# Hybrid mixer layer: the indexer's two query projections move into the modulation loop, the rotary tables ahead of it

## The chip, the cores and the metric

The kernel runs on one core of one Trainium2 chip. The metric is the device time of one execution in microseconds; lower is better. The core has five instruction streams that the profile names PE (TensorE, the matrix engine, with PEld for its weight loads), DVE (VectorE), ACT (ScalarE), POOL (GpSimd) and SP (here the queue that issues every DMA). Each works its queue strictly in order; an instruction that waits holds all that stand behind it.

## What is computed

One layer: a gated mixer of four causal branches on the same normalised and modulated input, and a gated convolutional feed-forward part. Sequence and width are 1024. For this change the first part of the mixer matters:

```python
mod = c_act @ ada_w[l] + ada_b[l]
sh1, sc1, g1, sh2, sc2, g2 = [m[:, None, :] for m in jnp.split(mod, 6, axis=-1)]
h = rmsnorm(x, mix_pre_g[l]) * (1.0 + sc1) + sh1
...
z = h @ w_in          # q, k, v of three attentions, conv input, qi, ki, wi, gates
...
q = rope(q, pos); k = rope(k, pos); qi = rope(qi, pos); ki = rope(ki, pos)
logits = jnp.einsum('bqhd,bkd->bqhk', qi[:, t0:t1], ki[:, :kl]).astype(jnp.float32) * IDX_HD ** -0.5
score = jnp.einsum('bqhk,bqh->bqk', jax.nn.relu(logits), wi[:, t0:t1])
score = jnp.where(jnp.arange(kl)[None, None, :] <= qpos[None, :, None], score, -jnp.inf)
_, idx = lax.top_k(score, topk)      # 256 keys for each query
```

The sparse attention then runs over the chosen keys alone. The indexer (qi, ki, wi) has eight heads of 32, so qi is 256 columns of `w_in`, two tiles of 128.

## The kernel before

All numbers stay in 32-bit precision by splitting: a matrix is written as a high and a low part (hH + hL for the input, whi + wlo for the weights), and a product is three matmuls, hH·whi, hL·whi and hH·wlo. `split_w` loads a weight tile of 128 columns (`wraw`), casts whi on ACT (L187) and subtracts on POOL to get wlo (L188). `proj` (L358) makes one tile: for each half of the sequence (512 positions) 24 matmuls, eight blocks of the contraction by three products, into one of the two buffers of `pmm`; then `consume` takes the half from PSUM. So one tile is 48 matmuls.

The program goes through these stages.

- **Head.** x comes in eight row tiles; each is scaled by its root mean square and transposed into xT (copies on DVE L313 and ACT L311). The modulation loop (L317) then has four steps m. In each, `ada_chunk` multiplies a 1024 x 512 piece of the modulation weights (four loads `adaw`, matmuls `adaps`, L205), ACT copies it (`adae`, L214), four small matmuls turn it into columns (`adac`, L217), and DVE forms `md`, A and B (L220 to L232). With these, two of the eight blocks of xT are scaled (DVE L320), cast to hH (ACT L322), and hL is the difference (DVE L323). After the loop come the rotary tables for two frequencies sets (`inv16`, `inv32`; DVE L326 to L338, sines on ACT L342 to L344) from the positions (`posi`).
- **Indexer.** `rope_tile` (L390) makes the two qi tiles: `proj`, two swapping copies on ACT (`sw`, L399 and L400), products with the tables on DVE (E=V; other rotary tiles use POOL), the cast `rhi` and the rest `lo` (kept in `sw`), and 16 row stores to a scratch in memory (`qk_s`, L123). `small_tile` (L416) makes ki together with wi; eight small transposes (`pw`, L453) need its `r`.
- **Scores.** For each of eight heads and six query blocks a score matmul (`sc<-kis,qis`, buffers `pss`, two of 1024), a relu on ACT and an accumulation on DVE. This part carries a higher priority than what stands behind it in the code.
- **Search.** A binary search over bits for the threshold of each query, on DVE (`search_v`, L607 to L620) and ACT (`search_a`, L634 to L638). Meanwhile TensorE works on the other projections: the plain tiles vc, vb, ua with the eight later modulation steps, then kdvd, qd, qc, kc, qb, kb. At its end DVE turns scores into masks (L674 to L679), and ACT writes them, one write for each of the query blocks 2 to 7 (`score<-key`, L680).
- **Sparse attention** (L690 to L730), in query blocks from 7 down: keys `kds` and queries `qds` are loaded from the scratch, score matmuls `sc<-kds,qds` (L468), maxima on DVE (`pd`, L710), exponentials on ACT (L719), transposes, and value matmuls (`av`, L488). Gate projections (32 tiles, `gate_tile`) fill TensorE from here on.
- **The rest**: stick-breaking attention with the causal convolution, differential attention, merge, and the feed-forward part.

No order is written out by hand. A scheduler places the instructions of all stages on the five queues, by priorities, by when buffers come free and by its own estimate of when each is ready; a change early in the program can therefore change the order far behind it.

## Time and profile before

| | us |
|---|---|
| median of 3 runs | 1996.43 |
| lowest, highest | 1993.14, 1999.46 |
| profiled execution | 1993.31 |
| span of its trace | 1991.5 |
| PE busy | 1809.1 (91% of the span) |
| DVE busy | 1284.8 (65%) |
| ACT busy | 913.2 (46%) |
| POOL busy | 770.3 (39%) |

The busy shares are means over stages that differ. Where a stage's limit lies is read from a window of the trace: the engine with hardly any idle time sets the pace there, and an engine with a hole in it tells in its timeline what it waited for. The timeline gives for each row the start, the duration, the engine, the line, the operation, the result and its sources, and in brackets the idle time ahead of it with what ended it.

### The profile page before, as it was taken

Reading aid. Unit: us, or ns where it says so; the run is one execution under the profiler, and the core shown is the slowest. Engines: PE = TensorE matmul, PEld = TensorE weight load, DVE = VectorE, ACT = ScalarE, POOL = GpSimd, SP = SyncE. Lnnn points to the kernel's source line nnn. Section 1 sums busy time; section 2 is a strip of 40 time slices with the busy share of each in tenths; the row PEclk is TensorE's granted clock in tenths of the full one; section 3 lists DMA queues with packets and bytes.
Section 4 is the critical chain, followed back from the end, with each engine's and each line's share of the span. In section 5 each row is a group of like instructions: output and inputs, shape, how many; then the busy total and the mean of one; then the engine's idle time right before and its main releaser. Section 6 shows DMA issues by size and latency. Waiting matters only on the chain.

```text
span 1991.5 us, 23311 instructions
## 1 busy us (share of the span) xinstructions
PE 1809.1 (91%) x8528; PEld 1403.5 (70%) x8528; DVE 1284.8 (65%) x1896; ACT 913.2 (46%) x1648; POOL 770.3 (39%) x425
## 2 busy tenths in 40 slices
PE   5888968399899999999999889869999999999998
PEld 3655656277677776767787667647888888778886
DVE  6758999704799865876313485577777777743532
ACT  5555757236546564555313344444444434343321
POOL 0202136273111111101214530198888888455450
PEclk9888989699999999989999989989999999999999
DMA  8355523343623224423223454312222222265631
GB/s 316 95 136 176 191 85 96 106 113 69 200 90 99 92 84 123 98 88 106 69 74 127 143 174 138 138 43 85 85 85 85 85 75 85 95 222 166 236 127 64
DMA packets 78306, 237.18 MB, mean 119 GB/s; under 512 B 10672, under 2 KB 14896, under 8 KB 78064
## 3 DMA queue, kind: packets, MB, share of 16 engines
q1 hardware_dynamic: 78192, 235.69, 36.9%
q8 instruction: 67, 1.10, 0.2%
q14 instruction: 47, 0.39, 0.1%
HBM read 179.82 MB, written 55.84 MB: 118 GB/s over the span
## 4 chain that ended last, share of the span: by engine, by line
PE 64%; DVE 21%; ACT 4%; issue 4%; POOL 3%; DMA 3%; SPq 0%; DVEq 0%; ACTq 0%; POOLq 0%
PE ups L963 19%; PE mm L367 18%; PE dps L1191 11%; DVE junkb L607 7%; PE brp L927 3%; PE av L488 3%; PE sc L468 3%; PE yps L1011 2%; DVE hc L874 2%; PE tr L478 2%; POOL wlo L188 1%; DMA x_s<-xt 1%; PE adaps L205 1%; DVE T L620 1%; DVE th L1101 1%
## 5 line engine op out<-in xcount | busy, mean ns | idle before, releaser
L188 POOL TENSOR_TENSOR wlo<-wraw,whi 128x1024 fp32r<-128x1024 f32 x104 | 267.5, 2577 | 858.5 <-ACT whi L187 822.3
L367 PE MATMUL mm<-hH,whi 128*128 128x512 f32 x864 | 356.6, 413 | 48.3 <-ACT whi L187 30.0
L367 PE MATMUL mm<-hH,wlo 128*128 128x512 f32 x864 | 352.0, 408 | 2.7 <-POOL wlo L188 2.6
L367 PE MATMUL mm<-hL,whi 128*128 128x512 f32 x864 | 353.8, 410 | 0.3 <-DVE hL L323 0.3
L963 PE MATMUL ups<-th,wblk 128*128 128x512 f32 x1320 | 316.0, 396 | 19.5 <-DVE ub L1143 7.4
L963 PEld LDWEIGHTS ups<-th,wblk 128*128 128x128 f32 x1320 | 251.2, 191 | 77.8 <-DVE th L1101 11.5
L367 PEld LDWEIGHTS mm<-hH,whi 128*128 128x128 f32 x864 | 168.1, 195 | 94.8 <-ACT whi L187 30.4
L367 PEld LDWEIGHTS mm<-hH,wlo 128*128 128x128 f32 x864 | 167.7, 194 | 41.5 <-POOL wlo L188 3.9
L187 ACT CAST whi<-wraw 128x1024 fp32r<-128x1024 f32 x122 | 127.4, 1048 | 148.2 <-DMA wraw<-in_w_dn 57.6
L367 PEld LDWEIGHTS mm<-hL,whi 128*128 128x128 f32 x864 | 168.6, 195 | 35.6 <-issue 2.6
L942 POOL TENSOR_TENSOR wblk<-wr,wblk 128x512 fp32r<-128x512 f32 x84 | 174.2, 2084 | 8.0 <-ACT wblk L941 8.0
L1205 DVE TENSOR_TENSOR actl<-actw,acth 128x512 fp32r<-128x512 f32 x42 | 65.0, 1573 | 105.1 <-ACT acth L1204 105.1
L607 DVE TENSOR_SCALAR_CACHE_REDUCE junkb<-key,cf 128x1024 bf16<-128x1024 uint16 (+3 forms) x124 | 117.3, 946 | 4.3
L963 PE MATMUL ups<-h2h,wblk 128*128 128x512 f32 x352 | 117.2, 395 | 0.0
L942 POOL TENSOR_TENSOR wblk<-wsum,wblk 128x512 fp32r<-128x512 f32 x66 | 100.0, 1517 | 35.8 <-ACT wblk L941 35.8
L1130 DVE SCALAR_TENSOR_TENSOR ub<-ub,pkt 128x1023 f32<-128x1023 f32 x44 | 64.1, 1458 | 67.7 <-ACT ub L1129 67.7
L1191 PE MATMUL dps<-wlo,acth 128*128 128x512 f32 x336 | 104.2, 390 | 2.1 <-POOL wlo L188 2.1
L1191 PE MATMUL dps<-whi,acth 128*128 128x512 f32 x336 | 104.0, 389 | 0.0
L941 ACT CAST wblk<-wr 128x512 fp32r<-128x512 f32 x88 | 54.3, 622 | 108.2 <-PE ups L963 83.7
L1191 PE MATMUL dps<-whi,actl 128*128 128x512 f32 x336 | 103.9, 389 | 0.0
L874 DVE SCALAR_TENSOR_TENSOR hc<-hpad,pkt,hc 128x1024 f32<-128x1024 f32 x60 | 84.3, 1409 | 0.0
L1132 DVE SCALAR_TENSOR_TENSOR ub<-ub,pkt 128x1022 f32<-128x1022 f32 x44 | 83.4, 1895 | 0.8
(591 smaller groups left out, 3422.4 us busy)
## 6 DMA issues: line engine op xcount, KB each, us to landing
wraw<-in_w_in SPq DMA_DIRECT2D x54, 512.0 KB, 3.9
adaw<-in_ada SPq DMA_DIRECT2D x48, 512.0 KB, 5.9
wr<-in_w_up SPq DMA_DIRECT2D x44, 512.0 KB, 3.4
wraw<-in_w_dn SPq DMA_DIRECT2D x44, 512.0 KB, 3.4
sg_s<-gt SPq DMA_DIRECT2D x44, 256.0 KB, 2.4
sgl<-sg_s SPq DMA_DIRECT2D x22, 512.0 KB, 3.4
act_s<-ub SPq DMA_DIRECT2D x22, 512.0 KB, 2.6
actw<-act_s SPq DMA_DIRECT2D x42, 256.0 KB, 4.2
```

The lines of the kernel that those rows point to most:

```text
L187: A.copy(hi, raw)
L188: (E or G).tensor_tensor(out=lo, in0=raw, in1=hi.bitcast(F32), op=OP.subtract)
L367: PE.matmul(ps, a[:, ks], b[:, k, cs], start=(n == 0), stop=(n == 3 * NK - 1))
L468: PE.matmul(ps[:, c0:c1], a, b[:, c0:c1], start=(si == 0), stop=(si == len(stacks) - 1 and not last))
L607: V.tensor_scalar(out=j[:, :n], in0=src, scalar1=scal, scalar2=None, op0=op, op1=OP.add, accum_out=dst[:, kc(t):kc(t) + 1])
L874: V.scalar_tensor_tensor(out=hc, in0=hpad[:, k:k + S], scalar=w(k), in1=hc, op0=OP.mult, op1=OP.add)
L942: E.tensor_tensor(out=b[:, 1], in0=r, in1=b[:, 0].bitcast(F32), op=OP.subtract)
L963: PE.matmul(ps, u[:, ks], v[:, k, :], start=(n == 0), stop=(n == 11))
L1130: V.scalar_tensor_tensor(out=u[:, 1:], in0=c[:, 0:S - 1], scalar=w(1), in1=u[:, 1:], op0=OP.mult, op1=OP.add)
L1132: V.scalar_tensor_tensor(out=u[:, 2:], in0=c[:, 0:S - 2], scalar=w(0), in1=u[:, 2:], op0=OP.mult, op1=OP.add)
L1191: PE.matmul(ps[:, cs], a[:, tl], b[:, cs], start=(chunk == 0 and n == 0 and i == 0), stop=(chunk == len(CH) - 1 and n == len(ops) - 1 and ...
L1205: V.tensor_tensor(out=lo, in0=raw, in1=hi.bitcast(F32), op=OP.subtract)
```

## The change

The loop over the four modulation steps moves behind the code of the rotary tables. Ahead of it the two qi weight tiles are split and two buffers of `pss` (the score banks) are taken. Within the loop, after each block j of hH and hL is made, 12 matmuls go into these two accumulators (two tiles, three products, two halves). `rope_tile` takes the finished accumulator in place of calling `proj`. The number of matmuls is the same.

```diff
             posi = stp.tile([P, S], I32, name="posi", tag="st")
             dma(posi, dap(pos, 0, [[0, P], [1, S]]))
-            for m in range(4):
-                mod_affine(m, A1, B1, "g1", pmm, "mm", stp, "st", adp)
...
             posf = stp.tile([P, S], F32, name="posf", tag="st")
...
                 tabs[kind] = (cs, sn)
 
+            qi_ps = []
+            for i in range(2):
+                qi_ps.append((pss.tile([P, S], F32, name="qips", tag="s"), split_w(w_in[W_INDEX[("qi", i)]])))
+            for m in range(4):
+                mod_affine(m, A1, B1, "g1", pmm, "mm", stp, "st", adp)
+                for j in (2 * m, 2 * m + 1):
+                    V.tensor_scalar(out=xT[:, j, :], in0=xT[:, j, :], scalar1=A1[:, j:j + 1],
+                                    scalar2=B1[:, j:j + 1], op0=OP.mult, op1=OP.add)
+                    A.copy(hH[:, j, :], xT[:, j, :])
+                    V.tensor_tensor(out=hL[:, j, :], in0=xT[:, j, :], in1=hH[:, j, :].bitcast(F32),
+                                    op=OP.subtract)
+                    ks = slice(j * P, (j + 1) * P)
+                    for ps, (hi, lo) in qi_ps:
+                        for n, (a, b) in enumerate(((hi, hH), (lo, hH), (hi, hL))):
+                            for hf in range(2):
+                                cs = slice(hf * 512, hf * 512 + 512)
+                                PE.matmul(ps[:, cs], a[:, ks], b[:, j, cs], start=(j == 0 and n == 0),
+                                          stop=(j == NK - 1 and n == 2))
...
-        def rope_tile(name, i, kind, nh, hd, scale=None, E=G):
+        def rope_tile(name, i, kind, nh, hd, scale=None, E=G, done=None):
...
-            proj(name, i, consume)
+            if done is None:
+                proj(name, i, consume)
+            else:
+                for hf in range(2):
+                    cs = slice(hf * 512, hf * 512 + 512)
+                    consume(hf, cs, done[:, cs])
             store_hl(name, i, hi, lo, nh, hd, True)
...
-            rope_tile("qi", i, "inv16", 4, 32, E=V)
+            rope_tile("qi", i, "inv16", 4, 32, E=V, done=qi_ps[i][0])
```

What this moves on the queues is seen at three places. The number behind a name tells one buffer from the next, and "..." stands for rows left out. Lines of the changed kernel are 11 to 16 higher from L318 on: L354 is the new matmul, L378 `proj`, L410 to L419 `rope_tile`, L484 a score matmul, L552 `hl_tile`, L696 the score write.

**TensorE in the modulation.** Before, the four steps follow each other; the first projection matmul (mm_494) stands behind the last:

```order
L217 MATMUL adac_321<-ones_66,adae_319 128x1 x4
L205 MATMUL adaps_337<-adaw_338,cst_c_99 32x512
...
L217 MATMUL adac_356<-ones_66,adae_354 128x1 x4
L205 MATMUL adaps_372<-adaw_373,cst_c_99 32x512
...
L217 MATMUL adac_391<-ones_66,adae_389 128x1 x4
L205 MATMUL adaps_407<-adaw_408,cst_c_99 32x512
...
L217 MATMUL adac_426<-ones_66,adae_424 128x1 x4
L367 MATMUL mm_494<-hH_117,whi_490 128x512
```

After:

```order
L217 MATMUL adac_365<-ones_66,adae_363 128x1 x4
L205 MATMUL adaps_405<-adaw_406,cst_c_99 32x512
...
L354 MATMUL qips_332<-hH_117,whi_335 128x512 x2
...
L354 MATMUL qips_339<-hL_118,whi_342 128x512 x2
L217 MATMUL adac_424<-ones_66,adae_422 128x1 x4
L205 MATMUL adaps_464<-adaw_465,cst_c_99 32x512
...
L354 MATMUL qips_332<-hH_117,whi_335 128x512 x2
...
L217 MATMUL adac_483<-ones_66,adae_481 128x1 x4
```

Between each two groups of adac there are now 24 matmuls of the two qi tiles, on the blocks that the step made.

**TensorE ahead of the scores.** Before, the last tile ahead of the first score matmul is the second plain tile (vc, block 1; mm_1175 and mm_1201 are its halves):

```order
L367 MATMUL mm_1175<-hH_117,whi_1171 128x512
...
L367 MATMUL mm_1201<-hH_117,whi_1171 128x512
...
L367 MATMUL mm_1201<-hH_117,wlo_1172 128x512
L468 MATMUL sc_774<-kis_766,qis_771 128x384
L468 MATMUL sc_779<-kis_766,qis_771 128x512
```

After, the third plain tile (vb, block 0; mm_1263 and mm_1289) follows it ahead of the scores:

```order
L378 MATMUL mm_1199<-hH_117,whi_1169 128x512
...
L378 MATMUL mm_1199<-hH_117,wlo_1170 128x512
L378 MATMUL mm_1263<-hH_117,whi_1259 128x512
...
L378 MATMUL mm_1289<-hH_117,whi_1259 128x512
...
L378 MATMUL mm_1289<-hH_117,wlo_1260 128x512
L484 MATMUL sc_772<-kis_764,qis_769 128x384
```

So 48 matmuls moved from behind the first score matmuls to ahead of them.

**ACT at the end of the search, and SP at the start of the sparse attention.** ACT before, from the last instruction of its search (T2) on; chi_2115 is kc, block 0:

```order
L638 ACTIVATE T2_2702<-Bn_2705 128x2
L680 ACTIVATE score_759<-key_2695,zcol_68 128x384
L536 ACTIVATE chi_2115<-mm_2151 128x512
...
L680 ACTIVATE score_759<-key_2695,zcol_68 128x896
L187 CAST whi_2187<-wraw_2185 128x1024
L187 CAST whi_2255<-wraw_2253 128x1024
L680 ACTIVATE score_759<-key_2695,zcol_68 128x1024
```

ACT after; chi_2181 is qc, block 1, and sw_2318 is qb, block 0:

```order
L654 ACTIVATE T2_2700<-Bn_2703 128x2
L552 ACTIVATE chi_2181<-mm_2217 128x512
...
L187 CAST whi_2253<-wraw_2251 128x1024
L187 CAST whi_2322<-wraw_2320 128x1024
L696 ACTIVATE score_757<-key_2693,zcol_68 128x384
...
L696 ACTIVATE score_757<-key_2693,zcol_68 128x896
L410 ACTIVATE sw_2318<-mm_2326 64x512
...
L696 ACTIVATE score_757<-key_2693,zcol_68 128x1024
```

Two weight casts moved from behind five score writes to ahead of all, and the projections are one tile further. SP before, around the last query load (qds) and the row stores of the last four rotary tiles (rhi, sw):

```order
L123 DMA qds_3435<-qk_s_81 64x1024 x2
...
L123 DMA wraw_6482<-in_w_in 128x1024
L123 DMA qk_s_81<-rhi_2321 16x1024 x8
...
L123 DMA qk_s_81<-rhi_2594 16x1024 x8
L123 DMA qk_s_81<-sw_2593 16x1024 x8
L123 DMA o_s_85<-oT_3438 128x1024
```

SP after:

```order
L123 DMA qds_3433<-qk_s_81 64x1024
L123 DMA qk_s_81<-rhi_2319 16x1024 x8
...
L123 DMA qk_s_81<-rhi_2592 16x1024 x8
L123 DMA qk_s_81<-sw_2591 16x1024 x8
L123 DMA qds_3433<-qk_s_81 64x1024
L123 DMA wraw_6480<-in_w_in 128x1024
```

The second half of the last query load and the first gate weights (wraw_6480) moved from ahead of the 64 row stores to behind them.

## Rows read from the trace of the kernel before

**Rows 1.** Windows: from:to, length; busy us (xcount) by engine; granted clock, DMA share, GB/s.

```profile
31.00:47.00 16.00, 11.51 (x71) 5.31 (x71) 13.39 (x24) 8.27 (x10) 0.00 (x0) 0.89 0.96 365
51.30:56.40 5.10, 5.10 (x13) 3.96 (x12) 5.10 (x9) 0.70 (x1) 1.50 (x1) 0.50 0.72 258
354.00:379.40 25.40, 0.01 (x1) 0.01 (x1) 24.74 (x37) 6.11 (x9) 1.34 (x1) 0.50 0.36 103
379.40:456.00 76.60, 70.15 (x291) 56.26 (x292) 7.56 (x3) 26.81 (x40) 54.18 (x35) 0.94 0.47 111
560.00:600.00 40.00, 35.94 (x188) 26.86 (x187) 39.73 (x46) 19.19 (x37) 5.30 (x2) 1.00 0.20 67
```

**Rows 2.** Timeline of DVE, end of the search.

```profile
353.68 0.16 DVE L620 SCALAR_TENSOR_TENSOR T<-ge,T 128x4 f32<-128x4 f32 x1
```

**Rows 3.** Timeline of PE, from the search to the attention.

```profile
379.39 0.79 PE L367 MATMUL mm<-hH,whi 128*128 128x512 f32 x1 [29.96 <-ACT whi L187]
...
455.42 1.99 PE L468 MATMUL sc<-kds,qds 128*128 128x512 f32 x8
...
465.47 1.97 PE L488 MATMUL av<-aT,vd 128*64 128x128 f32 x32
```

**Rows 4.** Timeline of ACT, score writes and the first rotary tile behind the search.

```profile
377.36 1.04 ACT L680 ACTIVATE score<-key,zcol 128x896 f32<-128x896 bf16 x1 [4.16 <-DVE key L679]
...
387.06 1.15 ACT L680 ACTIVATE score<-key,zcol 128x1024 f32<-128x1024 bf16 x1 [6.78 <-DVE key L679]
...
412.75 0.59 ACT L399 ACTIVATE sw<-mm 64x512 f32<-64x512 f32 x1 [3.65 <-PE mm L367]
```

**Rows 5.** Timeline of PE, two modulation steps.

```profile
30.03 1.05 PE L217 MATMUL adac<-ones,adae 128*128 128x1 f32 x8 [0.73 <-ACT adae L214]
...
35.22 1.05 PE L217 MATMUL adac<-ones,adae 128*128 128x1 f32 x8 [2.08 <-ACT adae L214]
```

**Rows 6.** Timeline of DVE, last x copy, modulation, tables.

```profile
25.94 0.69 DVE L313 COPY xT<-xtr 128x512 f32<-128x512 f32 x1 [1.31 <-PE xtr L308]
...
31.84 1.53 DVE L320 TENSOR_SCALAR xT<-xT,A,B 128x1024 f32<-128x1024 f32 x2
...
47.87 2.71 DVE L330 TENSOR_SCALAR ang<-posf,pkt 128x1024 f32<-128x1024 f32 x1
...
54.21 0.74 DVE L330 TENSOR_SCALAR ang<-posf,pkt 128x1024 f32<-128x1024 f32 x1
...
56.31 1.21 DVE L336 SCALAR_TENSOR_TENSOR ang<-kk,ang 128x1024 f32<-128x1024 f32 x1
```

**Rows 7.** Timeline of ACT, hH casts of a step and a sine.

```profile
32.69 1.99 ACT L322 CAST hH<-xT 128x1024 fp32r<-128x1024 f32 x2 [2.71 <-DVE xT L320]
...
63.91 1.15 ACT L342 ACTIVATE sininv<-ang,pkt 128x1024 f32<-128x1024 f32 x1 [0.69 <-DVE ang L338]
```

**Rows 8.** Chain that ended last, around M: start, length, what.

```profile
444.30 11.28 PE mm L367 x48
...
459.12 4.49 ACT pd L719 x8
```

**Rows 9.** Timeline of PE, second query projection.

```profile
69.39 0.79 PE L367 MATMUL mm<-hH,whi 128*128 128x512 f32 x1 [4.41 <-DVE r L402]
```

**Rows 10.** Timeline of POOL, weight remainders of the two qi tiles.

```profile
47.29 5.51 POOL L188 TENSOR_TENSOR wlo<-wraw,whi 128x1024 fp32r<-128x1024 f32 x2 [46.85 <-ACT whi L187]
```

**Rows 11.** Timeline of ACT, the key tile's last r copy.

```profile
98.33 0.57 ACT L433 COPY r<-mm 32x512 f32<-32x512 f32 x1 [1.87 <-DVE r L428]
```

**Rows 12.** Timeline of POOL, two rotary products of the last tile.

```profile
470.92 2.77 POOL L407 TENSOR_TENSOR r<-r,sw 128x512 f32<-128x512 f32 x2
```

**Rows 13.** Timeline of SP, row stores of the last rotary tile.

```profile
482.03 3.86 SPq L123 DMA_DIRECT2D qk_s<-rhi  x8
485.99 4.26 SPq L123 DMA_DIRECT2D qk_s<-sw  x8
```

**Rows 14.** Page, DMA issues: count, size, median us to landing.

```profile
wraw<-in_w_in SPq DMA_DIRECT2D x54, 512.0 KB, 3.9
```

More of the change, by code (lines that the diff above doesn't have):

```diff
@@ L316, in tile_hybrid_block @@
             dma(posi, dap(pos, 0, [[0, P], [1, S]]))
-            for m in range(4):
-                mod_affine(m, A1, B1, "g1", pmm, "mm", stp, "st", adp)
-                for j in (2 * m, 2 * m + 1):
-                    V.tensor_scalar(out=xT[:, j, :], in0=xT[:, j, :], scalar1=A1[:, j:j + 1],
-                                    scalar2=B1[:, j:j + 1], op0=OP.mult, op1=OP.add)
-                    A.copy(hH[:, j, :], xT[:, j, :])
-                    V.tensor_tensor(out=hL[:, j, :], in0=xT[:, j, :], in1=hH[:, j, :].bitcast(F32),
-                                    op=OP.subtract)
             posf = stp.tile([P, S], F32, name="posf", tag="st")
```

## The prediction

> **What bounds the kernel now.** I read the windows first, whole engines by stage, then the timeline of each engine where a window shows a hole. [rows 1] gives five stretches. From 31 to 47 us, the modulation, TensorE is busy 11.5 of 16 us and the DMA engines 0.96 of the time. From 51.3 to 56.4, the start of the first query projection, TensorE runs at half clock. From 354.0 to 379.4, right after the threshold search, it does nothing (0.01 us). From 379.4 to 456.0, the last six projection tiles, it is busy 70.2 of 76.6. From 560 to 600 VectorE is the bound with 39.7 of 40. So the kernel is a row of stages with different limits, and a saving in one counts only until the next stage that waits for something else. For this change I follow three points: T, the end of the threshold search (353.7, DVE, [rows 2]); M, the first score matmul of the sparse attention (455.4); and the first value matmul behind it (465.5) [rows 3]. From T on TensorE waits 29.96 us for a weight cast on ACT that stands behind five score writes there [rows 3, 4].
>
> **The modulation with the projections in it.** Before, four modulation steps follow each other on TensorE at 5.2 us (30.03 to 35.22, [rows 5]), and the two indexer projections (96 matmuls) come behind. After, the tables go first, and each next step's column matmuls (adac) stand behind 24 projection matmuls that need this step's hH and hL.
>
> The tables: per kind four plain passes, taken like the 0.74 of the product, and three fused steps of 1.21, so 6.6 us; with the int cast 13.9 for both [rows 6]. They can begin when the x copies end (25.94 + 0.69), so the first modulation column is used at about 41, where the first xT scaling began at 31.84 before [rows 6]: +10 at the columns. ACT's sines (1.15 each, four, and two absolute values, [rows 7]) stand ahead of and between the first hH casts, another 2 to 3 us; the first projection matmul can start at about 45. TensorE has been idle for over 10 us by then, so it begins at half clock, 0.43 us a matmul (12 in 5.1 us, [rows 1]): 14 of them slow (6.1 us, as in the trace), ten at 0.235 (11.28/48, [rows 8]), ends 53.5. Each further step is adac (1.05, [rows 5]), the four small DVE operations (0.7), one xT scaling (0.77, half of 1.53, [rows 6]), one hH cast (1.0, half of 1.99, [rows 7]) and 24 matmuls (5.6): 9.2 us. Three of them end at 81. In the kernel before the second tile began at 69.39, slow after a wait [rows 9], and its 48 matmuls, some ten at 0.43, end at about 82.5: the overlap is taken back by the tables and by the chain that now runs through TensorE, and the gain is some **1.5 us**. The weights are no limit: their two loads now stand right behind x.
>
> POOL's two weight remainders move with them, from 47.29 (5.51 us, [rows 10]) to beside the x scaling and the tables. The row of 47.87 shows what that does: the table product took 2.71 us beside POOL and 0.74 alone [rows 6]. Twice 2.0 is at most +4; VectorE has some 2.3 us of gaps among its last x copies, so I count +1 to +2 and have put it into the 41 above. The Trainium skill, page "SBUF — State Buffer", section "Who interferes with whom", says that VectorE and GpSimd share a port pair as an exclusive lock, so that the later one is fully blocked; the trace agrees (2.71 for 0.74), and by that rule alone, with no gaps to hide in, the sum below would be 2 us higher.
>
> **From the indexer to the scores.** The key tile (48 matmuls, 11.3 us, [rows 8]) then ends at about 92. The order on ACT now has the two r copies of this tile behind all six sw copies; the last one ended at 98.9 before ([rows 11], 5 us after the tile's last matmul), and 17 matmuls of the next tile stood between the two groups of transposes that need them. Now all eight transposes stand within the first two matmuls of that next tile, so TensorE waits 5 us at least, 6.6 with the six copies first (to about 98.5), and loses 2 more to the slow clock. And the order moves one whole plain projection tile (vb, block 0) ahead of the first score matmul: 48 matmuls, 11.3 us. Together −1.5 + 6.6 + 2 + 11.3 = 18.4, less some 1.4 of small waits of before in that stretch: the first score comes **+17 us** (+11 to +19). The scores are bound by VectorE and ACT, and the search by VectorE, so neither gets shorter: T moves by +17 too.
>
> **From T to M.** The tile that was moved ahead is missing behind the search: five tiles are left, not six, and the order puts the weight casts ahead of the score writes on ACT, so the 29.96 us wait goes. What is late next is the evacuation of the tiles between the score writes. The first half of the first rotary tile is evacuated behind the write of block 6, which ended at 377.36 + 1.04 = T + 24.7 [rows 4]; so at T + 25.5, where it was at 412.75 = T + 59.1. From there to M was 42.7 us (412.75 to 455.42). Its second half stands behind the write of block 7 (387.06 + 1.15 = T + 34.5) and the table load, some 11 us after the first, where 24 matmuls alone need 5.6 (half of 11.28, [rows 8]): +1 to +5, and I take +4. M is at T + 72 (25.5 + 42.7 + 4), before T + 101.7: **−30 us**.
>
> **From M to the attention.** On SP the second half of one query load (qds) and the next gate weights now stand behind the 16 row stores of the last rotary tile. Before, all query loads were issued ahead of those stores, and the stores went at 482.03 and 485.99, when nobody waited. TensorE's queue has a score matmul on that load in front of the value matmuls, and ACT has the cast of the gate weights in front of the next exponential, so both stand. The chain: the first exponential began at M + 3.7 and the value matmuls at M + 10 [rows 3, 8], so the first transposes are copied at an estimated M + 6.5 and the two r copies behind them end at M + 7.5; POOL's four pairs of rotary operations 5.4 (twice 2.7, [rows 12]); rhi and lo 1.9 until the stores can go on; 16 issues 3.86 + 4.26 = 8.1 [rows 13]; the load behind them 3.9 [rows 14]; the cast 1.0; then exponentials to the first value matmul 6.4 (459.12 to 465.47). That is M + 34 to 36, where it was M + 10.05: **+25 us**. No row of before shows SP's queue in that state, so the bounds are 0 (the load split lands before anyone needs it) and +30 (POOL locked beside VectorE's maxima, each operation like the 2.71 above).
>
> **Behind it** nothing is added: the same gate matmuls (1536) remain, some 28 more of them done when the first value block ends, and in the stretch from 560 on VectorE is the bound [rows 1], which takes what is left over. I count 0, with −5 to +3.
>
> **The sum:** +17 − 30 + 25 = +12. The profiled execution took 1993.31 us (span 1991.5), 3.1 below the median; on the median the forecast is 1996.4 + 12 = **2008**. Its own range is 2002.5 to 2018, from +23 to +27 for the stall, T + 69 to T + 74 for M, and 3 us either way at the head.
>
> **Rivals.**
> A faster one: the attention is not held. For it: no row of before shows the stall, it is read from SP's order alone, and a longer way to M would let the rotary work of the last tile go on before M. Against it: the POOL chain and the 16 issues stand ahead of the load and cannot be passed. It decides if the split load lands by about M + 10; then the 25 falls away: 2008 − 25 = 1983, and up to 1990 where part of it stays.
>
> A slower one: TensorE stays at half clock through the modulation steps. After each group of 24 matmuls it has only small matmuls until the next step. [rows 9] speaks for it: after an idle wait of 4.41 us the next projection began with 0.79 and 0.63 us matmuls, a granted clock of 0.5. Against it: the gap here is 3.6 us with eight modulation matmuls in it. It decides if each step starts slow: 24 at 0.43 in place of 0.235 is +4.7, three times, +14: 2022. The Trainium skill, page "TensorE: Matmul & The Clock Gate", section "HAM oscillation — how this bites in real kernels", describes just that, each short group starting cold after a wait; the trace agrees at 69.39, and no run here has the alternation yet.
>
> One without a difference: the head costs half. If the tables hide in the gaps of the x phase (they can start by tile, and x lands earlier when the modulation weights stand behind it), the first step is 5 us earlier, and the transposes find their copies in time (−5): +12 − 10 = 1998 to 2002.
>
> That the change does not do what it says is the case of the head itself: the projections do run inside the modulation, but their end moves by 1.5 us.
>
> **How the numbers follow.** Measurements of this kernel tell 0.3% from no change: 1990.4 to 2002.4. My forecast has 0.46, the slow clock 0.12, the head at half cost 0.19, the attention not held 0.23. Faster comes from the last alone, slower from the first two and a little of the third: faster 0.23, same 0.20, slower 0.57. To leave out no more than 2 in 10 the range must reach to the attention that isn't held and to the slow clock: 1981 to 2024.
>
> **What would show it.** In the new profile: the first projection matmul near 45 and the last near 81, in steps of about 9 us; the first score matmul about 17 us later; no hole in TensorE behind T; M at T + 72; then a hole of over 20 us in TensorE before the first value matmul, released by the query load. I am wrong if the steps are much shorter than 9 us, if the score matmuls start less than 8 us later, or if that hole is not there.

## The result, and the profile after

The changed kernel takes **2010.58 us** (median of six runs, 2005.66 to 2012.05); the kernel before takes 1997.13 in the runs beside it. The ratio is 1.0067 with a 95% interval of 1.0052 to 1.0081: slower by 13.4 us. The profiled execution of the changed kernel has a span of 2009.7 us, 18.2 more than before; the 4.8 us between the two differences come from the executions that were profiled (before's lies 3.8 under its median, after's 0.9 over).

The windows of the changed kernel, cut at its own first score matmul, end of the search, first score matmul M of the sparse attention and first value matmul; the next is the stretch of [rows 1] from 560; the last is everything behind the last gate tile. Columns as in [rows 1], with PE first and the granted clock after POOL.

```profile
0.00:139.86 139.86, 102.89 (x480) 75.92 (x481) 67.82 (x123) 57.80 (x91) 16.18 (x14) 0.90 0.53 167
139.86:382.96 243.10, 203.11 (x806) 138.31 (x805) 226.05 (x452) 159.25 (x375) 80.33 (x65) 0.87 0.45 149
382.96:456.63 73.67, 58.02 (x222) 45.00 (x220) 33.09 (x39) 26.97 (x40) 44.92 (x29) 0.91 0.35 76
456.63:494.05 37.42, 14.41 (x56) 10.40 (x54) 11.08 (x24) 12.48 (x21) 14.68 (x10) 0.64 0.60 164
...
560.00:600.00 40.00, 38.30 (x215) 28.46 (x214) 36.94 (x60) 18.38 (x52) 5.50 (x2) 1.00 0.43 125
963.40:2009.70 1046.30, 988.09 (x4237) 796.62 (x4235) 589.65 (x646) 396.67 (x591) 559.86 (x286) 0.98 0.33 114
```

The last row is the first thing to see: 1046.3 us, and behind the last gate tile of the kernel before it is 1045.9. By that tile is meant the last of the 22 gate tiles that run ahead of the merge (ten more follow in it); its milestone is the start of ACT's last copy of it. So the whole loss is made up to that tile, and up to there both kernels issue the same matmuls. T is the start of the search's last operation. The milestones (us from the span's start):

| | first score | T | M | first value matmul | last gate tile | span |
|---|---|---|---|---|---|---|
| before | 120.5 | 353.7 | 455.4 | 465.5 | 945.0 | 1991.5 |
| after | 139.9 | 382.8 | 456.6 | 494.1 | 962.8 | 2009.7 |
| difference | +19.4 | +29.1 | +1.2 | +28.6 | +17.8 | +18.2 |

TensorE in the changed kernel, the head and then the attention, with the wait and its end in brackets:

```profile
43.19 1.22 PE L354 MATMUL qips<-hH,whi 128*128 128x512 f32 x2 [8.88 <-ACT hH L346]
...
50.95 0.95 PE L217 MATMUL adac<-ones,adae 128*128 128x1 f32 x8
...
54.60 0.73 PE L354 MATMUL qips<-hH,whi 128*128 128x512 f32 x2 [0.83 <-ACT hH L346]
...
60.20 0.95 PE L217 MATMUL adac<-ones,adae 128*128 128x1 f32 x8
...
69.46 0.95 PE L217 MATMUL adac<-ones,adae 128*128 128x1 f32 x8
73.10 1.22 PE L354 MATMUL qips<-hH,whi 128*128 128x512 f32 x2 [2.70 <-ACT hH L346]
...
80.82 0.63 PE L354 MATMUL qips<-hL,whi 128*128 128x512 f32 x2
...
100.28 0.64 PE L469 MATMUL pw<-ctile,r 32*128 32x32 f32 x4 [6.24 <-ACT r L449]
...
393.74 0.80 PE L378 MATMUL mm<-hH,whi 128*128 128x512 f32 x1 [4.27 <-ACT czf L553]
...
456.63 1.31 PE L484 MATMUL sc<-kds,qds 128*128 128x512 f32 x5
...
481.81 1.62 PE L484 MATMUL sc<-kds,qds 128*128 128x512 f32 x3 [18.25 <-DMA qds<-qk_s]
...
494.05 1.97 PE L504 MATMUL av<-aT,vd 128*64 128x128 f32 x32
```

The projections run from 43.19 to 81.3, in steps of 9.25 us (50.95, 60.20, 69.46). The transposes `pw` wait 6.24 us. The hole behind the search, 29.96 us [rows 3], is gone; 4.27 us at 393.74 is the longest in its place. M comes 73.8 us after T instead of 101.7. And in front of the value matmuls stands the hole of 18.25 us, released by the query load. SP's queue in that stretch shows who holds it:

```profile
470.36 3.54 SPq L123 DMA_DIRECT2D qk_s<-rhi  x8
474.31 3.67 SPq L123 DMA_DIRECT2D qk_s<-sw  x8
478.03 0.45 SPq L123 DMA_DIRECT2D qds<-qk_s  x1
478.52 0.58 SPq L123 DMA_DIRECT2D wraw<-in_w_in  x1
```

And ACT in the same stretch:

```profile
468.50 0.62 ACT L419 CAST rhi<-r 128x512 fp32r<-128x512 f32 x1 [3.32 <-POOL r L418]
...
482.94 1.04 ACT L187 CAST whi<-wraw 128x1024 fp32r<-128x1024 f32 x1 [12.61 <-DMA wraw<-in_w_in]
485.82 1.15 ACT L735 ACTIVATE pd<-pd,sm 128x1024 f32<-128x1024 f32 x1 [1.83 <-DVE sm L734]
```

SP waits for the last rotary tile, issues its 16 rows (470.36 to 478), and only then the query half and the gate weights. ACT waits 12.61 us for these weights with the second exponential behind them.

One thing was not foreseen. The end of the search on VectorE:

```profile
373.05 0.90 DVE L635 TENSOR_TENSOR ge<-cnt,kreq 128x4 f32<-128x4 f32 x1
373.99 2.29 DVE L636 SCALAR_TENSOR_TENSOR T<-ge,T 128x4 f32<-128x4 f32 x1
376.32 2.29 DVE L632 TENSOR_SCALAR cf<-T 128x4 f32<-128x4 f32 x1
...
382.80 0.16 DVE L636 SCALAR_TENSOR_TENSOR T<-ge,T 128x4 f32<-128x4 f32 x1
```

POOL at the same time:

```profile
373.90 4.68 POOL L188 TENSOR_TENSOR wlo<-wraw,whi 128x1024 fp32r<-128x1024 f32 x2
```

Operations of four columns, 0.16 us at 382.80 and at the end of the search before [rows 2], take 2.29 beside two weight remainders on POOL. The search has 93 such small operations (31 steps of three). Before, 12 of them last over 0.3 us, after, 23, and every one of these lies beside an instruction on POOL. They add up to 28.9 us before and 38.8 after, while the counting passes between them take 127.6 us in both, and the search is 8.0 us longer (180.6 to 188.6). The longest stands in the kernel before, beside three rotary operations of POOL:

```profile
301.72 3.73 DVE L620 SCALAR_TENSOR_TENSOR T<-ge,T 128x4 f32<-128x4 f32 x1
```

The Trainium skill, page "SBUF — State Buffer", section "Who interferes with whom", says that a VectorE operation with two inputs in this memory contends with a GpSimd operation that reads it, over a port pair that is an exclusive lock; the trace agrees for T, which has two such inputs and was held almost a whole POOL subtraction (2.29 us of 2.36). cf, which reads one tile, was held as long at 376.32.

### The profile page after: what moved, and what is told of

Its sections match the earlier page's. It is cut to its first block, busy times and chain, and to the rows that moved or that the text cites. A ratio compares the mean times of both kernels' runs of the same rounds, so it can differ in the third digit from the quotient of the medians.

```text
span 2009.7 us, 23319 instructions
## 1 busy us (share of the span) xinstructions
PE 1813.9 (90%) x8528; PEld 1405.3 (70%) x8528; DVE 1288.9 (64%) x1896; ACT 915.0 (46%) x1648; POOL 769.8 (38%) x425
## 4 chain that ended last, share of the span: by engine, by line
PE 62%; DVE 21%; DMA 4%; ACT 4%; POOL 4%; issue 3%; SPq 1%; DVEq 0%; ACTq 0%; POOLq 0%
PE ups L979 19%; PE mm L378 16%; PE dps L1207 11%; DVE junkb L623 7%; PE sc L484 3%; PE av L504 3%; PE yps L1027 2%; PE tr L494 2%; PE brp L943 2%; PE qips L354 1%; DVE hc L890 1%; SPq L123 1%; DMA x_s<-xt 1%; POOL wlo L188 1%; DVE ge L635 1%
## 5 line engine op out<-in xcount | busy, mean ns | idle before, releaser
L378 PE MATMUL mm<-hH,whi 128*128 128x512 f32 x832 | 344.8, 414 | 27.8 <-ACT r L415 12.2
L378 PE MATMUL mm<-hH,wlo 128*128 128x512 f32 x832 | 340.0, 409 | 2.4 <-POOL wlo L188 2.4
L378 PE MATMUL mm<-hL,whi 128*128 128x512 f32 x832 | 341.4, 410 | 0.0
L979 PE MATMUL ups<-th,wblk 128*128 128x512 f32 x1320 | 314.3, 394 | 21.1 <-DVE th L1117 8.0
L378 PEld LDWEIGHTS mm<-hH,whi 128*128 128x128 f32 x832 | 162.1, 195 | 74.3 <-ACT r L415 15.0
L187 ACT CAST whi<-wraw 128x1024 fp32r<-128x1024 f32 x122 | 127.6, 1048 | 169.3 <-DMA wraw<-in_w_dn 56.7
L378 PEld LDWEIGHTS mm<-hH,wlo 128*128 128x128 f32 x832 | 161.4, 194 | 42.2 <-issue 5.8
L378 PEld LDWEIGHTS mm<-hL,whi 128*128 128x128 f32 x832 | 162.4, 195 | 34.2 <-issue 3.4
```

The source lines that it names most:

```text
L187: A.copy(hi, raw)
L378: PE.matmul(ps, a[:, ks], b[:, k, cs], start=(n == 0), stop=(n == 3 * NK - 1))
L979: PE.matmul(ps, u[:, ks], v[:, k, :], start=(n == 0), stop=(n == 11))
```

## The experiments

The theory, A: the change costs by what the scheduler's order did far behind it, namely the plain tile that it put ahead of the scores (later T) and the row stores that it put ahead of the query load and gate weights (the hole); and the head gains nothing since tables and chain eat the overlap. The rival, B: what such an order does is taken up elsewhere, by the work that is left over up to the gates, so that undoing it gives next to nothing, and the loss lies in the head. Their milestones in one table (profiled executions; ratio of the times to the kernel before that ran beside each, with interval). They come from one execution each, which lies 4.9 us over the median in e3, 5.8 over it in e6 and 3.7 under it in e7. In e2 and from e5 on the search's last operation lasts 2.29 us, so that the search ends 2.1 us later, against the other rows, than T says.

| | first score | T | M | value | last gate | us | ratio |
|---|---|---|---|---|---|---|---|
| after | 139.9 | 382.8 | 456.6 | 494.1 | 962.8 | 2010.6 | 1.0067 [1.0052, 1.0081] |
| e1 stores last | 138.6 | 379.7 | 455.1 | 478.4 | 952.3 | 2003.1 | 1.0033 [1.0022, 1.0043] |
| e2 tile back | 127.1 | 355.5 | 436.3 | 472.8 | 942.7 | 1990.2 | 0.9959 [0.9944, 0.9974] |
| e3 tables behind | 130.9 | 368.6 | 471.7 | 481.7 | 962.7 | 2007.3 | 1.0052 [1.0034, 1.0070] |
| e4 tables ahead | 119.6 | 355.4 | 457.2 | 467.3 | 946.8 | 1995.3 | 0.9998 [0.9986, 1.0010] |
| e5 both undone | 126.6 | 357.7 | 435.8 | 454.2 | 936.5 | 1984.2 | 0.9950 [0.9938, 0.9962] |
| e6 r first | 128.5 | 357.0 | 437.8 | 472.9 | 943.6 | 1989.0 | 0.9973 [0.9962, 0.9984] |
| e7 columns first | 123.5 | 351.9 | 429.9 | 467.3 | 935.6 | 1985.8 | 0.9959 [0.9947, 0.9971] |
| e8 all | 121.6 | 348.3 | 427.9 | 446.3 | 928.6 | 1979.4 | 0.9924 [0.9912, 0.9936] |
| e9 casts behind | 127.4 | 356.3 | 434.3 | 450.6 | 931.1 | 1981.8 | 0.9929 [0.9911, 0.9947] |
| e10 all, r not first | 122.8 | 351.1 | 429.1 | 445.5 | 926.1 | 1976.4 | 0.9904 [0.9890, 0.9919] |

### e1: the last tile's stores behind the loads

An issue order alone: the 16 stores of the last rotary tile (kb, 1) go behind the last query load of the first pair, and behind the first weights of the gates loaded there.

```diff
+    def behind(late, early):
+        for i in late:
+            tc.add_manual_dep(i.ins, early.ins.name, nosync, reason="issue order")
+    behind(stores["kb", 1], first_gate_weight_load)
+    behind(stores["kb", 1], last_query_load_of_pair_0)
```

> The changed kernel, with the 16 row stores of the last rotary tile queued on SP behind the second half of the last query load and the first gate weights; nothing else moves ahead of the sparse attention. Theory A (what TensorE stands idle before the gate projections end is paid in full): the 18.25 us wait for the query load goes, the first value matmul comes at about 470 in place of 494, and the kernel takes 1990 (1986 to 1994). Theory B (the stages behind give such a hole back, since the lag against the kernel before shrank from 27.6 us at the end of the sparse attention to 9 at the end of stick-breaking): not under 2005.

It gave 7.5 us (2003.1), between the two, and the intervals of the ratios do not overlap: the order of the stores does cost time, less than half of what A said. ACT of this kernel shows why:

```profile
467.01 0.62 ACT L430 CAST rhi<-r 128x512 fp32r<-128x512 f32 x1 [3.33 <-POOL r L429]
468.23 0.62 ACT L430 CAST rhi<-r 128x512 fp32r<-128x512 f32 x1 [0.60 <-POOL r L429]
468.76 1.04 ACT L189 CAST whi<-wraw 128x1024 fp32r<-128x1024 f32 x1
```

TensorE behind it:

```profile
469.85 0.80 PE L380 MATMUL mm<-hH,whi 128*128 128x512 f32 x1 [6.50 <-ACT whi L189]
...
478.35 1.97 PE L515 MATMUL av<-aT,vd 128*64 128x128 f32 x32
```

M to the value matmul shrank from 37.4 to 23.2 us, not to the 10 of before. ACT still has two casts ahead of the weights that wait for POOL, and the stores of the tile before (qb, 1), SP 450.32 to 457.6, still stood ahead of the load.

### e2: the plain tile back behind the first score matmul

```diff
-                    plain_tile(name, i, dst, func)
+                    with (tc.issue_after(first_score.ins) if (name, i) == ("vb", 0) else ExitStack()):
+                        plain_tile(name, i, dst, func)
```

> The changed kernel, with the third plain tile (vb, block 0) queued behind the first score matmul again; the query load still stands behind the row stores. Theory A: the first score matmul comes at about 128.5 (now 139.9), the search ends some 11 us earlier, M comes at 446 to 452 (now 456.6), and the kernel takes 2003 (1999 to 2007). Theory B (its 48 matmuls are only moved, and TensorE has no room for them in the search): M stays at 455 to 458 and the time at 2010, within 3.

It took away more than A said: 20 us against the changed kernel, and it beats the kernel before. First score 127.1, near the 128.5 expected; but the search ends 25.2 us sooner (27.3 by T) where the first score comes 12.8 sooner, and M comes 20.4 sooner. The edit does not put the tile back where the kernel before had it. There its first matmul stands behind 74 of the 80 score matmuls:

```profile
162.98 0.77 PE L367 MATMUL mm<-hH,whi 128*128 128x512 f32 x1
```

In e2 it stands behind two of them, and its last behind 46, while the next plain tile takes the late place:

```profile
127.48 0.40 PE L378 MATMUL mm<-hH,whi 128*128 128x512 f32 x1
```

So the run takes the tile from ahead of the scores and fills TensorE's waits among them with it, where neither kernel had one. The window of this kernel's scores stage shows one part (the granted clock is the third number from the end):

```profile
127.08:178.00 50.92, 46.96 (x177) 26.28 (x175) 42.99 (x59) 36.74 (x54) 5.35 (x5) 0.93 0.66 207
```

The same stage in the kernel before:

```profile
120.50:173.00 52.50, 44.26 (x129) 23.61 (x128) 44.05 (x54) 37.15 (x53) 8.48 (x6) 0.80 0.58 182
```

TensorE's granted clock is 0.5, the lower of its two levels, for 20.5 us of this stage before and for 23.9 in the changed kernel (mean 0.78 from 139.86 to 194), while the score matmuls wait for ACT and VectorE. With the tile's matmuls between them it is so for 6.8 us, TensorE does 48 matmuls more, and the stage is 4.1 us shorter than in the changed kernel (50.3 against 54.4; 52.6 before). So a tile placed there costs nothing; placed ahead, its 11.3 us stand in front of the first score. That the clock makes the stage shorter is not shown: 3.2 of the 4.1 us lie in the first seven heads, at 0.97 against 0.76, but in e5, with the same order and 0.93, these heads take as long as in the changed kernel (42.2 and 42.5 us; 39.3 in e2). The other part is the search, 180.4 us long by the end of its last operation instead of 188.7: its small operations add up to 29.8 us instead of 38.8, since POOL's work falls elsewhere.

That e2 beats the kernel before is therefore no proof for the change: one tile more is done by the end of the scores than there. The same edit on the kernel before was not run.

### e3 and e4: one half of the change alone

e3 keeps the projections in the loop and puts the tables behind it again; e4 is the kernel before with only the tables moved ahead. The edit of e3:

```diff
-            for kind in ("inv16", "inv32"):
...
             for m in range(4):
...
+            for kind in ("inv16", "inv32"):
...
```

and e4, against the kernel before:

```diff
+            for kind in ("inv16", "inv32"):
...
             for m in range(4):
...
-            for kind in ("inv16", "inv32"):
...
```

> One half of the change alone: the projections run block by block within the modulation loop, the rotary tables stay behind it as in the kernel before. By its order neither the extra tile ahead of the scores nor the split query load is there. Theory A: the first step begins at 34, not 43, the last projection matmul ends near 70 (now 81), the first score matmul comes at 110 to 116 (before 120.5), and the kernel takes 1989 (1985 to 1994). Theory B (the chain through adac takes the whole overlap back, as in the changed kernel): 1997, within 3.

> The other half alone: the rotary tables ahead of the modulation loop, the two projections behind it as in the kernel before; by its order neither the extra tile nor the split load is there. Theory A: the first modulation column is used at about 39 in place of 31, but the second projection no longer waits for VectorE's tables (4.4 us) and the first score matmul comes at 120 to 126; the kernel takes 1999 (1996 to 2003). Theory B (the tables cost their 10 us at the head in full): 2007, and most of the changed kernel's loss would be the tables.

Tables ahead cost nothing (0.9998, 1995.3 us, just under A's range): the first score is 0.9 us earlier, the rest within 2 us of before. The projections in the loop without them lose nearly as much as the whole change, some 10 us, and neither theory had that. TensorE of e3:

```profile
65.42 1.22 PE L333 MATMUL qips<-hH,whi 128*128 128x512 f32 x2 [5.25 <-ACT hH L325]
...
80.52 0.80 PE L377 MATMUL mm<-hH,whi 128*128 128x512 f32 x1 [6.45 <-ACT whi L187]
...
101.43 0.63 PE L468 MATMUL pw<-ctile,r 32*128 32x32 f32 x4 [5.11 <-ACT r L448]
```

The last two projection matmuls begin at 73.45, 7.4 us sooner than in the changed kernel. But the tables (VectorE up to 73.4, sines on ACT up to 78.2) stand between that and the rotary tiles, the next tile's weight cast on ACT comes behind the sines, and `pw` is at 101.43, later than with the tables ahead (100.28). Both kernels have the hole of before behind the search (TensorE idle 32.0 us from T to M in either). Read from these queues, what is gained at the projections is paid at the tables: they must go in one place or the other, and the chain from the last column to the key tile is no shorter. The first score is 10.4 us later than before, and scores and search take 4.5 us longer.

### e5: tile back and stores late together

e2, with the stores of (qb, 1) and (kb, 1) behind the query loads, and those of (kb, 1) behind the gate weights, as in e1.

```diff
+    behind(stores["kb", 1], first_gate_weight_load)
+    behind(stores["qb", 1] + stores["kb", 1], last_query_load_of_pair_0)
```

> The changed kernel with the tile back behind the first score matmul (as e2) and the row stores of the last two rotary tiles behind the query load, the last tile's also behind the first gate weights (e1 had left the tile before ahead of the load, and its hole was still 9.6 us). Theory A (TensorE's idle time up to the end of the gate projections is paid in full): against e2 the first value matmul comes 24 us earlier behind M (at M + 11 to 13), some 5 us of it are lost again where the second pair's query loads now stand ahead of gate weights, and the kernel takes 1973 (1969 to 1979). Theory B (half of such a hole comes back behind, as the gain of e1 may be read): 1983 or more.

1984.2 us, 0.9950: 26 us faster than the changed kernel, 11 slower than A had, and within B (1983 or more). By the medians the two effects nearly add up (20.4 and 7.5, 26.4 together); by the ratios, each against the kernel before beside it, the stores add less (0.9959 in e2, 0.9950 here, with overlapping intervals). A's sum failed twice. M to the value matmul is 18.4 us and not 11 to 13, with the queries in time; and of the 18.1 us that it is shorter than in e2, 6.2 are left at the last gate tile. That most of such a hole comes back is what B said; the section on the prediction shows where. ACT holds the second exponential behind two casts that wait for POOL:

```profile
447.69 0.62 ACT L430 CAST rhi<-r 128x512 fp32r<-128x512 f32 x1 [3.38 <-POOL r L429]
448.94 0.62 ACT L430 CAST rhi<-r 128x512 fp32r<-128x512 f32 x1 [0.63 <-POOL r L429]
449.46 1.15 ACT L754 ACTIVATE pd<-pd,sm 128x1024 f32<-128x1024 f32 x1
```

### e6: the key tile's r copies ahead of its sw copies (on e2)

```diff
             def consume(hf, cs, ps):
+                A.copy(r[64:96, cs], ps[0:32])
                 A.copy(sw[0:32, cs], ps[32:64])
...
-                A.copy(r[64:96, cs], ps[0:32])
```

> e2 with the key tile's two r copies ahead of its six sw copies on ACT. If the eight small transposes wait for these copies alone (theory A): they come at 95 in place of 98.5, the first score matmul 3.5 us earlier (at 123.5), and the kernel takes 1987 (1984 to 1989). If DVE's products of that tile set the pace of what follows: no change, 1990, within 1.

No change that can be told from e2: 1989.0 against 1990.2. The transposes come 2.6 us sooner (95.9), the first score 1.5 later (128.54). TensorE waits less for the transposes (6.25 us in e2), but now for the next tile, where e2 has no wait behind the transposes up to the first score:

```profile
95.90 0.31 PE L469 MATMUL pw<-ctile,r 32*128 32x32 f32 x2 [1.95 <-ACT r L441]
...
104.16 0.80 PE L378 MATMUL mm<-hH,whi 128*128 128x512 f32 x1 [2.86 <-DVE r L446]
```

So what TensorE must do before the first score counts, not the wait in front of `pw` alone; and its granted clock in the head was lower in this execution (0.89 against 0.92).

### e7: the next columns ahead of the projections (on e2)

In the code the projections of step m−1 come behind the modulation matmuls of step m, so that the chain to the next hH runs beside them.

```diff
             for m in range(4):
                 mod_affine(m, ...)
+                if m:
+                    qi_blocks((2 * m - 2, 2 * m - 1))
                 scale and cast blocks 2m, 2m+1
-                24 projection matmuls of blocks 2m, 2m+1
+            qi_blocks((6, 7))
```

> e2 with the modulation in step by one: the next step's column matmuls are traced ahead of this step's 24 projection matmuls, so that the DVE and ACT chain of a step runs beside the projections of the step before. Theory A (the step is 9.2 us because chain and projections add up): steps of 6 to 6.5, the last projection matmul at 69 (79 in e2), the first score matmul at 118, the kernel 1981 (1977 to 1986). Theory B (something else sets the pace of the steps, loads of the modulation weights or DVE): steps of 8 or more and 1988 to 1991.

Between the two: steps of 8.5 us instead of 9.25, as B had them, the first score 3.6 us sooner than in e2, the time (1985.8) inside A's range and 4 us less by the medians, but the same ratio to the kernel before, so the gain is not shown in the time. TensorE:

```profile
53.98 1.94 PE L205 MATMUL adaps<-adaw,cst_c 128*32 128x512 f32 x16
...
55.85 0.73 PE L348 MATMUL qips<-hH,whi 128*128 128x512 f32 x2
...
56.88 0.95 PE L217 MATMUL adac<-ones,adae 128*128 128x1 f32 x8
```

The modulation matmuls of the next step stand behind the last group of projections that the queue had, and copy, columns, scaling and cast follow (hH at 59.43), so that chain still takes part of each step.

### e8: all of it

e7, with the one table that the indexer needs ahead of the loop and the other behind it, the r copies first as in e6, and the stores as in e5.

```diff
-            for kind in ("inv16", "inv32"):
+            def table(kind):
...
+            table("inv16")
...
             for m in range(4):
...
+            table("inv32")
```

> All of e5, e6 and e7 together, and of the tables only the indexer's own frequencies ahead of the loop, the other table behind it (7 us less on DVE ahead of the first step). If the gains add (theory A): the first projection matmul at 37, the first score matmul at 108 to 111, the kernel 1955 (1948 to 1964). If the head's gains are lost again at a common wait (theory B: the search ends no earlier, since scores and key tile wait for DVE's products): 1970 or more.

1979.4 us, 0.9924, faster than both kernels and on B's side. A's 1955 was not reached: the last two projection matmuls begin at 70.04 and `pw` at 88.84, 11.4 us sooner than in the changed kernel, but the first score, at 121.6, is only 5.5 sooner than in e2. TensorE of e8:

```profile
88.84 0.44 PE L490 MATMUL pw<-ctile,r 32*128 32x32 f32 x4
...
97.93 0.63 PE L390 MATMUL mm<-hH,whi 128*128 128x512 f32 x1 [2.87 <-DVE r L467]
```

The wait has moved from the transposes to the next tile, whose bank the key tile still holds.

### e9: two casts behind the second exponential (on e5)

Again an order alone: on ACT the two `rhi` casts of (kb, 1) go behind the exponential of pair 0, block 7, second head.

```diff
+                ex = A.activation(p_[:, :n], src[:, :n], AF.Exp, bias=sm[:, 1:2], accum_out=sm[:, 2:3])
+                if (pr, t, hh) == (0, NT - 1, 1):
+                    behind(rhi_casts["kb", 1], ex)
```

> As the run with both parts undone (the plain tile back behind the first score matmul, the last tile's stores behind the query loads), and in addition the two rhi casts of the last rotary tile stand on ACT behind the second exponential of the attention. In that run the second exponential began at 449.46, held by two casts that waited 3.38 and 0.63 us for POOL's r, while its scores were done some 5 us earlier. Theory A, the rest of the hole before the first value matmul is the order on ACT: the first value matmul comes 4 to 5 us sooner behind M (13.5 to 14.5 us instead of 18.4), and the time falls by 3 to 5 us, to 1979 to 1981 against 1984 (ratio about 0.993). Theory B, VectorE's maxima and POOL's rotary work beside each other hold it: M to the value matmul stays 17 to 19 us and the time stays at 1984 (0.995).

M to the value matmul fell by 2.0 us, to 16.4; the last gate tile came 5.4 us sooner. The time, 1981.8 against 1984.2, is 0.2% lower; the intervals (0.9911 to 0.9947 and 0.9938 to 0.9962) overlap, so the time alone doesn't settle it. ACT, the second exponential:

```profile
444.87 1.15 ACT L756 ACTIVATE pd<-pd,sm 128x1024 f32<-128x1024 f32 x1 [2.05 <-DVE sm L755]
```

TensorE, the first value matmul:

```profile
450.64 1.97 PE L519 MATMUL av<-aT,vd 128*64 128x128 f32 x32 [1.47 <-ACT aT L512]
```

The exponential now waits for VectorE's maximum (`sm`), not for the casts. So the order on ACT was part of the rest of the hole, less than the 4 to 5 us that A gave it; M to the value matmul was 10.05 us before, and the other 6 are not resolved.

### e10: all of it, with the r copies back and the casts late

e8 without the edit of e6, and with that of e9.

```diff
-                A.copy(r[64:96, cs], ps[0:32])
                 A.copy(sw[0:32, cs], ps[32:64])
...
+                A.copy(r[64:96, cs], ps[0:32])
...
+                    behind(rhi_casts["kb", 1], ex)
```

> As the run with all parts (columns first, half of the tables ahead, the plain tile back, the stores late), but the key tile's r copies stand behind its sw copies again, and the two rhi casts of the last rotary tile behind the second exponential. Theory A, the r copies in front delayed the key tile's rows and with them the first score: the first score comes at 117 to 119 (121.6 with them in front), the value matmul 4 us sooner behind M, time 1972 to 1975 (ratio 0.988 to 0.990). Theory B, the first score hangs on the tables of the key tile and not on this order, and the casts give nothing: first score at 121 to 125, time 1979 to 1981 (0.992).

1976.4 us, **0.9904**, the fastest here: 19 us less than the kernel before beside it (1995.8) and 34 less than the changed kernel. A's reason falls: without the r copies in front the first score is at 122.8 and not at 117 to 119. TensorE, as in e6, pays for the transposes or for the next tile:

```profile
94.79 0.63 PE L492 MATMUL pw<-ctile,r 32*128 32x32 f32 x4 [5.12 <-ACT r L472]
...
122.84 0.56 PE L509 MATMUL sc<-kis,qis 128*128 128x384 f32 x2
```

B's time (1979 to 1981) falls as well. The value matmul comes 16.3 us behind M, 2.1 less than in e8, as in e9.

## Why the prediction was right, step by step

The sign was right, and so were the mechanisms that it named: the overlap taken back, the tile ahead of the scores, the hole behind the search gone, the new one in front of the value matmuls. That the time came out within 3 us (2008 against 2010.58) is luck: up to the value matmul the sum is 16.6 us short (+12 against +28.6), behind it it is 10.4 too high, and the two cancel.

| step | predicted | measured |
|---|---|---|
| projections in the loop | from 45 to 81, steps of 9.2 | from 43.2 to 81.3, steps of 9.25 |
| wait of the transposes | 6.6, then slow | 6.24, then 0.63 us a pair up to 105.7 |
| first score | +17 | +19.4 |
| scores and search get longer by | 0 | +9.8 (scores 1.8, search 8.0) |
| T | +17 | +29.1 |
| T to M | 72 (−30) | 73.8 (−27.9) |
| M to the value matmul | 34 to 36 (+25) | 37.4 (+27.4) |
| sum at the value matmul | +12 | +28.6 |
| behind it | 0 (−5 to +3) | −10.4 |
| whole | +12 | +18.2 in the span, +13.4 in the medians |

**The head** came as worked out: the overlap of projections and modulation is taken back (TensorE is idle 37.0 us up to the first score, 26.3 before). e4 shows that the tables cost nothing where they were put when the projections stay behind, and e3 that the projections in the loop gain nothing when the tables don't go ahead. The term of +1 to +2 for POOL's remainders is in the trace (the position cast took 2.25 us beside them, 0.69 alone in the kernel before). Two sums of the forecast do not come out as said: 26.6 and 13.9 make 40.5, so that the 41 holds half a microsecond of that term, and the lower end of its own range, 2002.5, is not what the bounds beside it add up to (2000).

**The tile ahead of the scores** was costed at 11.3 us, and as a shift that the stretch behind the search gives back. It did so: T to M is 27.9 us shorter. What e2 adds is that among the score matmuls the same tile would have cost nothing.

**"Neither gets shorter"** left out that they can get longer, and is the first step that was mis-sized. The sum had VectorE's search as a fixed length; its 8 us more are small operations beside POOL, set by what POOL does in that stretch. The 1.8 us of the scores are not resolved.

**T to M and the hole** came as read from the order: no hole of 30 us, and a new one, by the row stores. e1 shows the stores as a cause (37.4 to 23.2 with them late); the terms of the chain, POOL's pairs, the stores, the load and the cast, are all there: 464.77, 470.36, 478.03, 482.94. What the prediction left out is that with the stores away the rest does not fall to 10: e5 and e9 stand at 18.4 and 16.4.

**"Behind it nothing"** is the second, off by 10.4 us. The forecast had some 28 gate matmuls more done by the first value block and gave them no worth. In fact, at the end of the sparse attention (546.5 us before, 574.1 after) 75 gate matmuls were done before and 118 after, 10 of these in front of the first value matmul; and the value stage took no longer for it (81.0 and 80.0 us), since they fill its waits (TensorE is idle 7.1 us in it before, 1.3 after). From there to the last gate tile the kernel before takes 398.5 us and the changed one 388.8. So the 43 matmuls come back as 9.7 us. The other runs bear it out: with 75 (e3, e4, e5, e8 to e10) that stretch takes 397.4 to 398.5 us, with 118 (e2, e6, e7) 388.3 to 389.9, with 102 (e1) 396.7. This is also, in part, why the late stores cost less than the hole that they make. VectorE, which the forecast had as the bound from 560 on, is busy 36.9 of 40 us there after, and TensorE 38.3.

**Counting another way** shows both. Up to the last gate tile TensorE does the same matmuls, so its end moves by TensorE's idle time and by how long it is busy with them. Idle: 128.0 us before, 137.6 after, by stage (to the first score, the end of the search, M, the value matmul, behind it):

| | head | to T | to M | to value | behind | sum | busy |
|---|---|---|---|---|---|---|---|
| before | 26.3 | 41.8 | 32.0 | 1.7 | 26.2 | 128.0 | 816.9 |
| after | 37.0 | 40.0 | 15.7 | 23.0 | 21.9 | 137.6 | 825.2 |
| e2 | 39.3 | 36.0 | 13.9 | 22.1 | 21.1 | 132.5 | 810.2 |
| e5 | 38.0 | 36.9 | 13.9 | 7.0 | 27.0 | 122.8 | 813.7 |

9.6 us of idle time and 8.3 of slower matmuls are the 17.8 at the last gate tile. The head is worth +10.7, and not the first score's +19.4: the moved tile is no loss in idle time. With the tile among the scores (e2) the idle time falls by 5.1 us and the busy time of the same matmuls by 15.0; the granted clock from the first score to the end of the search is 0.91 there, 0.87 in the changed kernel and 0.88 before.

**The rivals.** That the attention is not held is refuted by the 18.25 us. The half clock came in one step of the three: the 24 matmuls at 73.10 start slow after 2.70 us of waiting (granted clock 0.50 from 73.10 to 76.00), those at 54.60 after 0.83 us do not (1.00 from 54.60 to 60.20). In the first steps the modulation matmuls of the step after next stand in the gap, in the last there are none left; no run takes them away alone. The Trainium skill, page "TensorE: Matmul & The Clock Gate", section "HAM oscillation — how this bites in real kernels", has each short group start cold after a wait; here that holds for the group with nothing in its gap. It cost 12 matmuls some 0.2 us each, about 2.5 us, and not 14. The head at half its cost did not happen either.

## What to carry to other kernels

Where the engine that is most busy does the same work in both versions, count its idle time and its time at half clock up to the point from which nothing differs; a delay at a milestone is a loss only where no work was moved ahead in exchange. Before moving work forward look where the most busy engine waits anyway: among the waiting score matmuls a projection tile was free, ahead of them it cost its full time. And read the order of every queue far behind the edit. Moving the tile gave 20 us and the row stores 7.5, more than the 13.4 that were lost, since the new order had also taken away the wait of 29.96 us behind the search [rows 3].

With both mended (e5, e9, e10) the kernel is 0.5 to 1% faster than the one before, but the runs do not show that the idea itself, projections within the modulation, is what pays. In every run that has it the first score, after at least the same 432 matmuls, comes later than before (122.8 in e10, the best, against 120.5), and in e5 TensorE is idle 11.7 us longer up to there. The gain comes behind it: a tile in the scores' waits, and 18.1 us less idle time from the search to M, where ACT's weight casts no longer stand behind the score writes. Whether the kernel before gains as much with these two orders alone was not run.

## What the runs showed of the hardware

Operations of four columns on VectorE, 0.16 us alone, last 2.29 beside a subtraction of 128 x 1024 on POOL and up to 3.73 beside three rotary operations there; the search with 93 such operations became 8 us longer when more of them fell beside POOL's work (23 in place of 12 over 0.3 us). TensorE's granted clock among score matmuls that wait for other engines was 0.78 to 0.84 in the five kernels without a tile among them, and 0.90 to 1.00 in the seven with 48 projection matmuls between them; the stage took 52.4 to 54.8 us without and 50.0 to 50.8 with them, 53.1 in e5.
